# Side work of a hybrid decoder step resumed at estimated ready times, and x kept in scratch memory during the mixer

## The chip, the cores and the metric

The kernel runs on one core of one Trainium2 chip. It is one program that the core's engines work through in parallel: TensorE for matmuls (PE in the profile, with its weight loads as PEld), VectorE (DVE), ScalarE (ACT), GpSimd (POOL), and SyncE (SP), which issues most of the DMAs. Each engine takes its own instructions strictly in the order in which the program lists them, and waits where an operand isn't there yet. The metric is the device time of one execution in microseconds (us); lower is better.

## What is computed

One layer of a decoder for 512 prompt tokens and 8 sampled tokens (520 columns), in float32. Cut to what matters:

```python
def layer(x, ...):
    x = x + 0.5 * rmsnorm(swiglu(rmsnorm(x, ffn1_pre_g), gate1, up1, down1), ffn1_post_g)
    m, states = token_mixer(rmsnorm(x, mix_pre_g), ...)
    x = x + rmsnorm(m, mix_post_g)
    x = x + 0.5 * rmsnorm(swiglu(rmsnorm(x, ffn2_pre_g), gate2, up2, down2), ffn2_post_g)

def swiglu(x, w_gate, w_up, w_down):           # 1024 -> 2816 -> 1024
    return (silu(x @ w_gate) * (x @ w_up)) @ w_down

def token_mixer(h, ...):
    proj = h @ w_in                             # q, k, v, gates of two branches
    o_r = retention_chunked(rope(rq), rope(rk), rv)        # 4 heads of 128
    o_g = gated_delta_chunked(*conv_and_silu(conv_in))     # 4 heads of 128
    o_r = silu(rg) * normalized(o_r); o_g = silu(gz) * normalized(o_g)
    return (sigmoid(gate_r) * (o_r @ w_ret_branch) + sigmoid(gate_g) * (o_g @ w_gdn_branch)) @ w_out
```

The 8 sampled tokens go through the recurrent form of both branches: they read stored states, use them, and write them back updated.

## The kernel before, in words

**Matmuls.** Activations stand transposed, 128 channels by 520 tokens, in two halves of 260 columns. Each float32 product is made of three passes over numbers split into a high and a low part (L298 high by high, L299 high by low, L300 low by high; `passes`). These are the main stream: 9000 matmuls of 260 columns, whose order neither the tasks below nor the change touches. The names of their outputs tell the stage: `g` and `u` are the plain gate and up products at the start of an FFN, `sv` its further ones (seven products in place of eight for a pair of tiles), `dn` a down product or the mixer's output product, `p` the mixer's projections, `br` its branch products.

**Weights.** A weight tile is loaded to one of two `raw` buffers (L200 to L211, SP's queue), split on ACT (`whi`, L258) and on DVE or POOL (`wlo`, L259), for `sv` with `w` (L276, L277) from tiles of which some are first summed by POOL-issued DMAs that add in memory (L218). A `raw` buffer takes the next load when its `wlo` is done. SP's queue is in order: a load that waits for its buffer holds back every load and store behind it. I number the tiles ("units") of a stage from 0; `prefetch` splits about two units ahead, unless `hold` or `hold_sums` is set.

**Side work.** Everything else is written as generators: the RMS norms, the conv, the heads, the state updates. `tick()` is called after every second k-step of the main stream (6 matmuls) and advances every task whose step count has come: `yield 4` in a task means "resume four ticks later". So the place of a side instruction between the main matmuls is set by constants such as `yield 14` in `begin`, `yield 8` and `yield 13` in `gates`, `yield 9 + (0 if h else 6)` in `gdn_head`. They set the program's order only; what really happens on the chip is that an engine stops at an instruction whose operand is late.

**The RMS norm between two stages.** `post` finishes a stage: it gets the row sums by eight or four thin matmuls (`ss`, L360), a root on POOL (`rs`, L355), spreads it (`rb`, L366), and makes the new x half by half: DVE `t` (L492), POOL adds it to x (L494), ACT and DVE split it (`xhl`, L389, L390). `pre_rms` squares x (ACT, L407), adds the squares (DVE, L435) and starts `inverse_rms`: `ss` again, `ms` on DVE (L351), `rs`, sixteen `rb` in all, two copies (ACT L452, DVE L450). The result `r` scales every first product of the next stage when it leaves PSUM; the main stream begins that stage's products with `xhl` before `r` is there, and keeps them in PSUM banks (8 in all). `hold` is set in `post` and was cleared at the end of `pre_rms`, so that no weights are split in between except on demand; `hold_sums` is cleared at the end of `inverse_rms`.

**x.** x (8 tiles) stays in SBUF slots through the mixer, and is stored to a scratch tensor `x2` only for the second FFN, whose down stage loads it again (L623 in `down`, given `x_from`).

The functions in question, with the line numbers of the profile:

Of the kernel before, what the change touches and what calls it, by code (L numbers as in the profile page):

```python
# [7 lines left out]
F32 = mybir.dt.float32  # L8
# [7 lines left out]
P = 128  # L16
# [83 lines left out]

class Kernel:
    def __init__(self, ctx, tc, a):
        self.tc, self.nc, self.a = tc, tc.nc, a
        nc = tc.nc
        pool = lambda name, **kw: ctx.enter_context(tc.tile_pool(name=name, **kw))
        self.cpool = pool("const", bufs=1)
        self.big = pool("big", bufs=SLOTS)
        self.raw = pool("raw", bufs=RAW_BUFS)
        self.whl = pool("whl", bufs=SPLIT_BUFS)
        self.wk = pool("wk", bufs=2)  # L110
        self.sm = pool("small", bufs=8)
        self.ps = pool("ps", bufs=8, space=PSUM)
        self.dram = pool("scratch", bufs=1, space=DRAM)
        self.n = 0
        self.unit_list = units()
# [17 lines left out]
        self.loaded = {}  # L133
        self.split_done = {}
# [16 lines left out]
    def tick(self):  # L151
        self.now += 1
        self.add_sums()
        self.prefetch()
        for t in list(self.tasks):
            if t[0] <= self.now:
                try:
                    t[0] = self.now + (next(t[1]) or 1)
                except StopIteration:
                    self.tasks.remove(t)  # L160

# [28 lines left out]

    def load_to(self, j):

        nc, a = self.nc, self.a
        while self.raw_next < min(self.group[min(j, len(self.unit_list))] + RAW_BUFS, self.group[-1]):
            u = self.unit_list[self.first_of[self.raw_next]]
            if u[0] == "seven":
                w, m = a[f"gu{u[1]}"], u[2]
                t = self.raw.tile([P, KD, P], F32, tag="raw", name=self.name("raw"))
                s1, s3, a22 = (self.slot(x, (P, KH, P)) for x in ("s1", "s3", "a22"))
                nc.sync.dma_start(out=t, in_=w[2 * m])  # L200
                nc.sync.dma_start(out=s1, in_=w[2 * m + 1, :, 0:KH])
                nc.sync.dma_start(out=s3, in_=w[2 * m, :, 0:KH])
                nc.sync.dma_start(out=a22, in_=w[2 * m + 1, :, KH:KD])

                self.sums_due.append((self.now + SUM_LAG, self.raw_next, s1, w[2 * m + 1, :, KH:KD]))
                self.sums_due.append((self.now + SUM_LAG, self.raw_next, s3, w[2 * m + 1, :, 0:KH]))
                t = [t[:, 0:KH], s3, None, a22, t[:, KH:KD], s1, None]
            else:
                kind, m, k0, k1 = u
                t = self.raw.tile([P, k1 - k0, P], F32, tag="raw", name=self.name("raw"))  # L210
# [160 lines left out]
    def rstd(self, acc, scale, wait, plus, meanwhile=None):  # L371
# [39 lines left out]
    def pre_rms(self, xs, r, plus):  # L411
# [15 lines left out]
        yield 2  # L427
        yield from self.inverse_rms(sq[0], r, plus)
        self.hold = False
# [7 lines left out]
    def inverse_rms(self, acc, r, plus):  # L437
# [7 lines left out]
        yield 2  # L445
# [11 lines left out]
    def post(self, y, acc, hf, gnext, xs, r, plus, plus_next):  # L457
# [5 lines left out]
        yield 1  # L463
        meanwhile = (lambda: self.clear.append(1)) if hf else (lambda: self.prefetch(True, 1))
        r2 = yield from self.rstd(
            acc, 1.0 / D, 2 if gnext is None else 3, plus and plus[0:PW, hf * PIECES : (hf + 1) * PIECES], gnext is not None and meanwhile or None
# [242 lines left out]
    def run(self):  # L709
# [44 lines left out]
        def begin():  # L754
            yield 14
# [4 lines left out]
        xs, r = self.mixer(xs, r, plus2)  # L760
        x2 = self.dram.tile([P, KD, TOK], F32, name="x2")

        def keep():
            while len(xs[1]) < KD or r[1] is None:
                yield 1
            for k in range(KD):
                nc.sync.dma_start(out=x2[:, k, :], in_=self.x[k])
                yield 1

        self.spawn(keep())  # L770
        self.ffn(PLAIN[2], xs, r, V_G2PRE, self.gh[:, 8:16], None, plus2, None, x2)
        self.finish()

    def load_first(self):

        nc, a = self.nc, self.a
        t = self.raw.tile([P, KD, P], F32, tag="raw", name=self.name("raw"))
# [15 lines left out]
    def mixer(self, xs, r, plus_next):  # L793
# [33 lines left out]
        self.dec_done = set()  # L827
        tiles, gate, lead = {}, {}, {}
# [70 lines left out]
        return self.down(yx, (8,), self.vec[:, V_MPOST : V_MPOST + 8], V_G2PRE, 3, None, plus_next)  # L899
# [42 lines left out]
    def gates(self, rows):  # L942

        nc, c = self.nc, self.cpool
        yield 4
# [14 lines left out]
        yield 8  # L960
# [23 lines left out]
        yield 13  # L984
# [69 lines left out]
    def silu_later(self, t):  # L1054
        yield 5
        self.nc.scalar.activation(t, t, AF.Silu)

# [276 lines left out]
    def finish_head(self, kind, h, sg):  # L1334

        nc = self.nc
        yield 1
        nc.scalar.activation(sg, sg, AF.Silu)
        sgd = self.cpool.tile([P, DEC], F32, name=self.name("sgd"))
        yield 2  # L1340
# [4 lines left out]
        yield 6  # L1345
# [20 lines left out]
    def rsqrt(self, src, n, scale, name, out):  # L1366

        nc = self.nc
        ps = self.bank("cs")
# [5 lines left out]
        yield 5  # L1375
# [5 lines left out]
    def broadcast_rows(self, cols, name):  # L1381

        nc = self.nc
        pt = self.bank("tr32")
# [5 lines left out]
        return d  # L1390

    def state_update(self, rows, k, src, decay, out):

        nc = self.nc
        for i in range(8):
# [6 lines left out]
            yield 14  # L1402
            decay(s, h, b0)
            yield 4
# [12 lines left out]
    def state_products(self, src, rhs, n):  # L1417
# [4 lines left out]
        yield 10  # L1422
        for i in range(8):
            s, nxt = nxt, self.load_state(src, i + 1) if i < 7 else None
            ps = self.bank("sp")
# [3 lines left out]
            yield 7  # L1429
        self.prod = acc  # L1430

    def decode_ret(self):
# [7 lines left out]
        acc = self.prod  # L1440
        t = c.tile([P, H, DEC], F32, name="rdo")
# [5 lines left out]
        yield 2  # L1447
# [4 lines left out]
        yield 2  # L1452
# [4 lines left out]
        rows = self.broadcast_rows(v.rearrange("p h b -> p (h b)"), "vrow")  # L1457
        yield 6
# [6 lines left out]
    def decode_gdn(self):  # L1465
# [17 lines left out]
        yield 6  # L1483
# [9 lines left out]
        tt(qk, kn, kq[:, :, :, 1], ALU.mult)  # L1493
        yield from self.state_products(self.a["sgdn"], lambda h, b: kq[:, h, b, :], 2)
# [14 lines left out]
        yield 4  # L1509
# [4 lines left out]
        rows = self.broadcast_rows(u.rearrange("p h b -> p (h b)"), "urow")  # L1514
        yield 6
# [119 lines left out]
```

## Time and profile before

| | |
|---|---|
| device time, three runs | 1293.72, 1294.5, 1299.86 us (median 1294.5) |
| the profiled execution | 1299.34 us, of which its span is 1297.3 us |
| PE busy, instructions | 1233.3 us (95%), x10061 |
| DVE busy | 866.5 us (67%), x1911 |
| ACT busy | 547.0 us (42%), x1127 |
| POOL busy | 317.2 us (24%), x410 |
| moved by DMA | 167.38 MB, mean 129 GB/s |

Times in views of the trace count from the span's start. In a row of the timeline the columns are start, duration, engine, line, operation, output<-inputs, shape, how often, and in brackets how long the engine had been idle and what ended that. A row of a table by stretches gives the stretch, its length, then busy time of PE, PEld, DVE, ACT and POOL, each with its number of instructions, then the granted clock of TensorE as a share of full speed, the share of the DMA engines and GB/s. A row of waits gives engine, output and line, what it waited for, total us, times, longest us. In the profile's list of DMA issues a row ends with the size of one and its median time from issue to landing.

The stages in the trace: first FFN from 0 to about 379 us, mixer to about 892, second FFN to the end.

### The profile page before, as it was taken

To read this page: it belongs to the slowest core of one execution; us is meant where nothing else is said; L and a number is where in the kernel's file an instruction comes from. 1 tells how busy PE (TensorE), PEld (TensorE's weight loads), DVE (VectorE), ACT (ScalarE), POOL (GpSimd) and SP (SyncE) were. 2 spreads that over 40 slices of the span, in tenths; PEclk is the share of its full clock that TensorE was granted. 3 is DMA by queue.
4 is the path that set the end of the run, shared out by engine and by line. 5 is a ranking of instruction groups with operands and counts; after the bars stand their busy time and mean duration, and the time that the engine had idled before them with its cause. 6 is when DMAs were issued, how large, how long until landed. Compare 5 with 4: busy or idle time off the path is not lost.

```text
span 1297.3 us, 25497 instructions
## 1 busy us (share of the span) xinstructions
PE 1233.3 (95%) x10061; PEld 1219.7 (94%) x10061; DVE 866.5 (67%) x1911; ACT 547.0 (42%) x1127; POOL 317.2 (24%) x410
## 2 busy tenths in 40 slices
PE   8899999999998997999999999998889999999995
PEld 7899999999988997989999999998889999999995
DVE  8888888642254887877687655446768887862334
ACT  6566655522233553212333343323546655542220
POOL 4111211000024359227512333403311111100003
PEclk8999999999997999899999999997889999999997
DMA  5677777243321233232333564321377777634321
GB/s 172 170 182 195 177 185 178 86 156 92 97 62 53 95 101 89 71 101 97 106 133 111 178 205 136 126 82 50 119 192 183 180 196 182 147 90 156 90 74 66
DMA packets 77127, 167.38 MB, mean 129 GB/s; under 512 B 14544, under 2 KB 20016, under 8 KB 77008
## 3 DMA queue, kind: packets, MB, share of 16 engines
q1 hardware_dynamic: 64432, 140.95, 33.9%
q0 software_dynamic: 12576, 24.81, 10.9%
q8 instruction: 79, 1.29, 0.4%
q14 instruction: 40, 0.33, 0.1%
HBM read 156.03 MB, written 9.70 MB: 128 GB/s over the span
## 4 chain that ended last, share of the span: by engine, by line
PE 71%; DVE 11%; POOL 5%; issue 4%; DMA 4%; ACT 3%; SPq 1%; POOLq 0%; ACTq 0%; DVEq 0%
PE sv L298 10%; PE sv L299 10%; PE sv L300 10%; PE dn L299 7%; PE dn L298 7%; PE dn L300 7%; PE p L298 4%; PE p L300 4%; PE p L299 4%; DVE wlo L259 2%; DMA s<-gu_in 2%; DVE cv L1048 1%; PE br L298 1%; PE br L299 1%; PE br L300 1%
## 5 line engine op out<-in xcount | busy, mean ns | idle before, releaser
L298 PE MATMUL p<-xhl,whi 128*128 128x260 f32 x784 | 237.5, 303 | 2.2 <-ACT whi L258 2.2
L300 PE MATMUL p<-xhl,wlo 128*128 128x260 f32 x784 | 227.8, 291 | 1.8 <-DVE wlo L259 1.0
L299 PE MATMUL p<-xhl,whi 128*128 128x260 f32 x784 | 228.3, 291 | 0.7 <-DVE xhl L390 0.6
L299 PE MATMUL dn<-hl,whi 128*128 128x260 f32 x704 | 199.6, 283 | 3.3 <-DVE hl L606 3.3
L298 PE MATMUL dn<-hh,whi 128*128 128x260 f32 x704 | 199.5, 283 | 0.0
L300 PE MATMUL dn<-hh,wlo 128*128 128x260 f32 x704 | 198.8, 282 | 0.0
L298 PE MATMUL sv<-th,w 128*128 128x260 f32 x608 | 173.2, 285 | 4.4 <-ACT u L638 4.3
L299 PE MATMUL sv<-tl,w 128*128 128x260 f32 x608 | 172.9, 284 | 0.0
L300 PE MATMUL sv<-th,w 128*128 128x260 f32 x608 | 172.9, 284 | 0.0
L298 PEld LDWEIGHTS p<-xhl,whi 128*128 128x128 f32 x784 | 154.5, 197 | 3.1 <-ACT whi L258 2.4
L259 DVE TENSOR_TENSOR wlo<-raw,whi 128x1024 fp32r<-128x1024 f32 (+2 forms) x107 | 116.4, 1105 | 60.4 <-ACT whi L258 60.0
L300 PEld LDWEIGHTS p<-xhl,wlo 128*128 128x128 f32 x784 | 154.1, 197 | 2.3 <-DVE wlo L259 1.2
L299 PEld LDWEIGHTS p<-xhl,whi 128*128 128x128 f32 x784 | 154.3, 197 | 1.6 <-DVE xhl L390 1.1
L258 ACT CAST whi<-raw 128x1024 fp32r<-128x1024 f32 (+2 forms) x137 | 126.7, 943 | 65.5 <-DMA raw<-dn_in 55.2
L218 POOL DMA_DIRECT2D s<-gu_in x76 | 67.1, 954 | 322.6 <-DMA s<-gu_in 149.1
L277 DVE TENSOR_TENSOR w<-s,w 128x512 fp32r<-128x512 f32 x152 | 104.5, 689 | 53.2 <-ACT w L276 52.1
L299 PEld LDWEIGHTS dn<-hl,whi 128*128 128x128 f32 x704 | 132.6, 188 | 4.1 <-DVE hl L606 4.1
L298 PE MATMUL sv<-xhl,w 128*128 128x260 f32 x456 | 129.4, 284 | 4.2 <-DVE t L617 4.2
L300 PEld LDWEIGHTS dn<-hh,wlo 128*128 128x128 f32 x704 | 132.6, 188 | 0.0
L298 PEld LDWEIGHTS dn<-hh,whi 128*128 128x128 f32 x704 | 132.6, 188 | 0.0
L299 PE MATMUL sv<-xhl,w 128*128 128x260 f32 x456 | 129.0, 283 | 0.0
L300 PE MATMUL sv<-xhl,w 128*128 128x260 f32 x456 | 128.9, 283 | 0.0
(362 smaller groups left out, 2990.8 us busy)
## 6 DMA issues: line engine op xcount, KB each, us to landing
raw<-gu_in SPq DMA_DIRECT2D x49, 512.0 KB, 3.7
raw<-win_in SPq DMA_DIRECT2D x49, 512.0 KB, 3.5
s<-gu_in SPq DMA_DIRECT2D x76, 256.0 KB, 4.2
s<-gu_in POOLq DMA_DIRECT2D x76, 256.0 KB, 4.8
raw<-dn_in SPq DMA_DIRECT2D x32, 448.0 KB, 3.5
a<-gu_in SPq DMA_DIRECT2D x38, 256.0 KB, 4.6
raw<-dn_in SPq DMA_DIRECT2D x16, 512.0 KB, 3.6
x<-x SPq DMA_DIRECT2D x16, 260.0 KB, 6.3
```

Source lines behind the costliest of these rows:

```text
L218: self.nc.gpsimd.dma_start(out=out, in_=term, accum_op=ALU.add)
L258: self.nc.scalar.copy(hi[:, ks], t[:, ks])
L259: eng.tensor_tensor(lo[:, ks], t[:, ks], hi[:, ks].bitcast(F32), ALU.subtract)
L277: nc.vector.tensor_tensor(w[:, 1], t[i], w[:, 0].bitcast(F32), ALU.subtract)
L298: mm(ps, hi[:, k, :], xh, start=first, stop=False, skip_group_check=more)
L299: mm(ps, hi[:, k, :], xl, start=False, stop=False, skip_group_check=more)
L300: mm(ps, lo[:, k, :], xh, start=False, stop=last, skip_group_check=more)
L1048: nc.vector.scalar_tensor_tensor(out=acc, in0=cin[:, j : j + SEQ], scalar=w[:, j : j + 1], in1=acc, op0=ALU.mult, op1=ALU.add)
```

## The change

A class `Clock` sees every instruction while the program is built. It keeps, with constants for each engine, an estimate of when each engine comes free and when each tile is written. `at(tiles)` gives the estimated ready time of tiles; a task that yields it is resumed by `tick` once the estimate of PE's time has reached it. `raw_tile` tells it when SP's queue has to wait for a `raw` buffer. Most fixed counts before an instruction of PE become such times. Nothing of it runs on the chip: what changes there is the order of the instructions.

```diff
+class At(float):
+    step = 1 << 30
+class Clock:
+    FIXED = {"DVE": 75.0, "ACT": 110.0, "POOL": 160.0}
+    TAIL = 90.0
+    COLUMN = {"DVE": 1.04, "ACT": 0.79, "POOL": 2.2}
+    HANDOVER = 120.0
...
+    def note(self, ins):
...
+        start = max([self.free[engine]] + [self.ready(x) + self.HANDOVER for x in args])
...
+        elif engine == "PE":
+            self.count += 1
+            full = all("float32r" in str(x.dtype) for x in args)
+            self.free[engine] = start + (cols / 2.4 + 11.0 if full else max(60.0, 4 * cols / 2.4))
+            end = self.free[engine] + 170.0
+        else:
+            column = 1.35 if ins.opcode == "TensorScalarPtr" and len(args) > 2 else self.COLUMN[engine]
+            self.free[engine] = start + self.FIXED[engine] + column * cols
+            end = self.free[engine] + self.TAIL
...
     def tick(self):
...
+        clock = self.clock
+        if clock.count == self.seen:
+            clock.free["PE"] += 300.0
+        self.seen = clock.count
         for t in list(self.tasks):
-            if t[0] <= self.now:
+            if t[0] <= clock.free["PE"] or t[0].step <= self.now if isinstance(t[0], At) else t[0] <= self.now:
                 try:
-                    t[0] = self.now + (next(t[1]) or 1)
+                    wait = next(t[1])
+                    t[0] = wait if isinstance(wait, At) else self.now + (wait or 1)
...
+    def at(self, *aps, within=None):
+        t = At(max(self.clock.ready(x) for x in aps) + self.clock.HANDOVER)
...
     def rstd(...):
-        yield wait
+        yield self.at(r[0:PW])
     def pre_rms(...):
         self.add_squares(1)
-        yield 2
+        self.hold = False
+        yield self.at(sq[0])
         yield from self.inverse_rms(sq[0], r, plus)
-        self.hold = False
     def inverse_rms(...):
-        yield 2
+        yield self.at(s[0:PW])
     def begin():
-        yield 14
+        yield self.at(self.sq[0])
     def gates(...):
-        yield 4
+        yield self.at(rows[0:8])
...
-        yield 8
+        yield self.at(ga, gb)
...
-        yield 13
+        yield self.at(beta, g)
     def silu_later(self, t):
-        yield 5
+        yield self.at(t)
     def gdn_head(...):
-        yield 9 + (0 if h else 6)
+        while k.name not in self.silued or q.name not in self.silued:
+            yield 1
+        yield self.at(k, q)
     def rsqrt(...):
+        yield self.at(src)
         ps = self.bank("cs")
     def state_products(...):
-        yield 10
+        yield 4
         for i in range(8):
             s, nxt = nxt, self.load_state(src, i + 1) if i < 7 else None
+            yield self.at(s)
...
-            yield 7
+            yield 4
     def run(self):
...
-        xs, r = self.mixer(xs, r, plus2)
-        x2 = self.dram.tile([P, KD, TOK], F32, name="x2")
+        x1, x2 = (self.dram.tile([P, KD, TOK], F32, name=n) for n in ("x1", "x2"))
+        self.spawn(self.keep(x1, xs, r))
+        xs, r = self.mixer(xs, r, plus2, x1)
+        self.spawn(self.keep(x2, xs, r))
```

The same is done in `finish_head`, `broadcast_rows`, `state_update`, `decode_ret`, `decode_gdn` and at the start of `post`. The heads' inner steps (`ret_head`, `inverse`, the chunk loop of `gdn_head`) keep their counts. `keep` stores the eight x tiles to `x1` after the first FFN, and the mixer's output stage loads them back (16 more DMAs of 260 KB); nothing else is added to or taken from any engine.

What it does to the order is shown at two places. The first is the end of the norm between the first FFN and the mixer, on ACT (units 2, 3, 4 and 5 of the mixer's weights are `whi` in this order; `early` is an evacuation, `rb` the copy of the first half of `r`). Before:

```order
L407 ACTIVATE sq_4827<-x_3865 128x260
L258 CAST whi_5101<-raw_4696 128x256 x4
L542 COPY early_4907<-p_5020 128x260
L452 COPY rb_5160<-rb_5161 128x260
L258 CAST whi_5179<-raw_4916 128x1024
L258 CAST whi_5185<-raw_5111 128x1024
L258 CAST whi_5215<-raw_5183 128x1024
```

And on ACT with the change:

```order
L503 ACTIVATE sq_4821<-x_3865 128x260
L354 CAST whi_5097<-raw_4696 128x256 x4
L354 CAST whi_5122<-raw_4925 128x1024
L638 COPY early_4916<-p_5029 128x260
L354 CAST whi_5143<-raw_5107 128x1024
L354 CAST whi_5204<-raw_5126 128x1024
L548 COPY rb_5230<-rb_5231 128x260
```

The high parts of units 3, 4 and 5 now stand ahead of the copy of `r`. POOL follows: its low parts of units 3 and 4 stood behind the root `rs`, and now stand ahead of it; on DVE the low part of unit 5 has moved from behind the copy L450 to just ahead of it. On PE the second `ss` stands 36 main matmuls later and the `rb` 48 later. At the norm between mixer and second FFN it is 36 and 42 (POOL's `wlo` of unit 3 ahead of `rs`, and on DVE the `wlo` of unit 4 ahead of `ms`).

The second place is on DVE in the second FFN, where the first weights of the `sv` products are split (`w`, `s`) between the token sums (`xd`, `ta`, `tb`, `tl`: four groups). Before:

```order
L571 TENSOR_TENSOR tl_11717<-tb_11694,th_11716 128x520
L606 TENSOR_TENSOR hl_11703<-h_11585,hh_11702 128x520
L259 TENSOR_TENSOR wlo_11722<-raw_11634,whi_11721 128x1024
L277 TENSOR_TENSOR w_1901_11733<-raw_11640,w_1901_11733 128x512
L277 TENSOR_TENSOR w_1904_11746<-s_1875_11642,w_1904_11746 128x512
L272 SCALAR_TENSOR_TENSOR s_1905_11749<-s_1874_11641,raw_11640 128x512
L277 TENSOR_TENSOR w_1906_11751<-s_1905_11749,w_1906_11751 128x512
L562 TENSOR_TENSOR xd_11764<-x_3861 128x260
```

And on DVE with the change:

```order
L662 SCALAR_TENSOR_TENSOR tb_11720<-x_10901,vec,tb_11720 128x260
L713 TENSOR_TENSOR t_11728<-early_11370,rb_11705 128x260
L373 TENSOR_TENSOR w_1896_11740<-raw_11597,w_1896_11740 128x512
L373 TENSOR_TENSOR w_1897_11743<-s_1867_11599,w_1897_11743 128x512
L368 SCALAR_TENSOR_TENSOR s_1898_11746<-s_1866_11598,raw_11597 128x512
L373 TENSOR_TENSOR w_1899_11748<-s_1898_11746,w_1899_11748 128x512
L667 TENSOR_TENSOR tl_11753<-ta_11719,th_11752 128x520
```

The block that reads the summed tiles stood behind the third of the four groups; now it stands inside the second, so one and a half groups more are behind it. On SP the loads for it now stand ahead of all eight stores to `x2`; before, one store stood ahead of them, five right behind, and two behind the next tiles' loads.

In the mixer, the thin matmul of the decode branch (`cs`, L1370) stands 36 main matmuls later, the four delta heads' chains 30 later; the sixteen groups of state products (`sp`) stand up to 48 later or up to 102 earlier.

More of the change, by code (lines that the diff above doesn't have):

```diff
@@ L114, in __init__ @@
         self.n = 0
+        self.clock = Clock()
+        nc.push_inst_callback(self.clock.note)
+        self.seen = 0
         self.unit_list = units()
@@ L188, in dbank, with raw_tile @@
         return self.bank(name)[:, 0:n]
+    def raw_tile(self, shape):
+        t = self.raw.tile(shape, F32, tag="raw", name=self.name("raw"))
+        self.raws.append(t)
+        if len(self.raws) > RAW_BUFS:
+            clock = self.clock
+            clock.free["SP"] = max(clock.free["SP"], clock.read.get(self.raws[-1 - RAW_BUFS].name, 0.0))
+        return t
     def load_to(self, j):
@@ L759, in run, with keep @@
         xs, r = self.ffn(PLAIN[1], xs, r, V_G1PRE, self.gh[:, 0:8], V_MPRE, plus1, None, a["xT"])
[L760 to L770 removed]
+        x1, x2 = (self.dram.tile([P, KD, TOK], F32, name=n) for n in ("x1", "x2"))
+        self.spawn(self.keep(x1, xs, r))
+        xs, r = self.mixer(xs, r, plus2, x1)
+        self.spawn(self.keep(x2, xs, r))
         self.ffn(PLAIN[2], xs, r, V_G2PRE, self.gh[:, 8:16], None, plus2, None, x2)
         self.finish()
+        nc.pop_inst_callback()
+    def keep(self, out, xs, r):
+        x = self.x
+        while len(xs[1]) < KD or r[1] is None:
+            yield 1
+        for k in range(KD):
+            self.nc.sync.dma_start(out=out[:, k, :], in_=x[k])
+            yield 1
     def load_first(self):
         nc, a = self.nc, self.a
[L777 removed]
+        t = self.raw_tile([P, KD, P])
         self.loaded[0] = t
```

92 lines of the change are left out of this document (70 added, 22 removed).

## The prediction

> **What bounds the kernel.** I read the totals first, then a table by stretches, then who PE waits for, and then the timeline around the longest waits.
>
> ```profile
> span 1297.3 us, 25497 instructions
> PE 1233.3 (95%) x10061; PEld 1219.7 (94%) x10061; DVE 866.5 (67%) x1911; ACT 547.0 (42%) x1127; POOL 317.2 (24%) x410
> PE 71%; DVE 11%; POOL 5%; issue 4%; DMA 4%; ACT 3%; SPq 1%; POOLq 0%; ACTq 0%; DVEq 0%
> ```
>
> PE is the bound: 64 us of the span are its idle time, and its share of the chain is 71%. But busy isn't the same as at full speed. The table by stretches shows where speed is lost:
>
> ```profile
> 0.00:62.00 62.00, 52.89 (x375) 50.65 (x376) 50.10 (x92) 37.07 (x79) 19.76 (x29) 0.89 0.64 178
> 62.00:372.00 310.00, 308.27 (x2572) 307.82 (x2572) 197.99 (x365) 142.28 (x274) 27.90 (x32) 1.00 0.54 146
> 372.00:420.00 48.00, 41.44 (x273) 40.07 (x273) 26.55 (x59) 18.93 (x44) 22.48 (x21) 0.79 0.16 48
> 420.00:490.00 70.00, 69.92 (x588) 69.49 (x588) 55.67 (x131) 38.07 (x95) 34.56 (x46) 1.00 0.30 92
> 490.00:585.00 95.00, 81.77 (x645) 79.53 (x645) 79.07 (x232) 26.75 (x60) 43.73 (x75) 0.91 0.30 91
> 585.00:700.00 115.00, 111.88 (x982) 109.57 (x982) 88.10 (x286) 36.50 (x82) 54.07 (x94) 0.99 0.34 108
> 885.00:965.00 80.00, 67.03 (x449) 64.69 (x449) 57.25 (x116) 39.25 (x87) 24.51 (x26) 0.81 0.41 116
> ```
>
> From 62 to 372 PE runs without a break: 310 us for 2572 matmuls, 0.12 us each, at full clock. Four stretches lose time: the start, the norm at 372 to 420, the mixer from 490 on, and the norm at 885 to 965. Who ends PE's waits:
>
> ```profile
> PE cs L1370 <- DVE gsq L1482: 5.6, 1, 5.6
> PE ss L360 <- DVE sq L435: 5.3, 2, 2.7
> PE sv L298 <- ACT u L638: 4.3, 2, 3.4
> PE sv L298 <- DVE t L617: 4.2, 1, 4.2
> PE sp L1427 <- DMA sd<-sret_in: 1.0, 1, 1.0
> PE ss L360 <- DVE sq L751: 0.9, 1, 0.9
> ```
>
> The first two are side instructions that stand on PE ahead of their operands, with main matmuls queued behind them. The change moves exactly these: both `ss` and the `cs` stand 36 main matmuls later. The next two are main matmuls that wait for a PSUM bank. No task's place can cure those unless DVE and ACT get there sooner.
>
> **The change, part by part.** The estimate runs while the program is built, and costs nothing on the chip. Each instruction of before is there again; 16 DMAs are added.
>
> *The norm after the first FFN.*
>
> ```profile
> 404.67 1.04 PE L360 MATMUL ss<-ones,sq 128*65 128x1 f32 x8 [2.66 <-DVE sq L435]
> 403.60:417.10 13.50, 12.43 (x61) 12.43 (x62) 1.54 (x5) 2.27 (x3) 6.34 (x3) 0.50 0.17 66
> 417.20:430.70 13.50, 13.50 (x115) 13.32 (x115) 9.71 (x23) 4.36 (x6) 0.67 (x4) 1.00 0.26 80
> 401.41 3.20 DVE L435 TENSOR_TENSOR sq<-sq,sq 128x260 f32<-128x260 f32 x7
> 405.99 1.64 POOL L355 TENSOR_TENSOR rs<-ms,mhalf 65x8 f32<-65x8 f32 x1 [7.11 <-DVE ms L351]
> 410.43 1.99 ACT L258 CAST whi<-raw 128x1024 fp32r<-128x1024 f32 x2
> 411.55 4.70 POOL L259 TENSOR_TENSOR wlo<-raw,whi 128x1024 fp32r<-128x1024 f32 x2 [3.92 <-ACT whi L258]
> 418.65 1.23 DVE L259 TENSOR_TENSOR wlo<-raw,whi 128x1024 fp32r<-128x1024 f32 x1 [6.36 <-ACT whi L258]
> 419.80 0.75 DVE L939 TENSOR_TENSOR rows<-early,rb 8x260 f32<-8x260 f32 x2
> ```
>
> PE stops at 402.0 for squares that are done at 404.6. Then the clock is 0.50 for 13.5 us, 61 instructions where the next 13.5 us hold 115. With the change PE does 36 main matmuls instead (4.3 us, to 406.3), by which time the squares are done: `ss` to 406.9, `ms` by 407.1. POOL is the doubtful step: `whi` of unit 3 can go at 401 (ACT is free, `hold` is cleared), its `wlo` takes 2.35 from 402.1; unit 4's raw load goes out as the squares begin, at 401.5, and needs 3.5 (below), `whi` to 406.1, `wlo` to 408.5, and only then `rs`, 1.64, to 410.1. PE reaches `rb` 24 matmuls after `ss`, at 409.8, so it waits 0.3 and ends the sixteen at 411.8. PE is then 48 matmuls further (5.7 us) at the same time as before, and at full clock where before ran at half until 417.1: 8 us.
>
> What is late next is DVE. It stood idle for 6.36 us to 418.65, because unit 5's `whi` waited for a raw buffer that POOL's late `wlo` held, and first uses `r` at 419.80. With the change unit 5 is loaded at 404.5 and split by 410.5, and DVE uses `r` from 412.3: 7.5 us sooner. From 420 to 490 DVE is busy 55.7 of 70, and the rest is a 0.7 us wait inside each conv, so it carries PE's lead no further than its own. I take **7.5**, with 3 to 8 as bounds.
>
> The clock is the larger part of that lead: 8 us at 0.50, of which PE's own wait is 2.66. The Trainium skill ("TensorE: Matmul & The Clock Gate", section "HAM oscillation — how this bites in real kernels") puts the rule as no PE-idle gaps over about 3.4 us. By that rule a gap of 2.66 us would not be enough; the half clock did begin with it here, so the row differs from the rule, and the row decides. What the rule leaves open is a rival below.
>
> *The mixer.*
>
> ```profile
> 489.24 0.29 DVE L1159 TENSOR_TENSOR cols<-se,rr 128x4 f32<-128x4 f32 x1 [3.19 <-POOL rr L1150]
> 514.04 0.17 DVE L1159 TENSOR_TENSOR cols<-se,rr 128x4 f32<-128x4 f32 x1 [1.71 <-POOL rr L1150]
> 516.99 0.23 DVE L1482 TENSOR_TENSOR gsq<-dcv 128x64 f32<-128x64 f32 x1 [0.35 <-ACT dcv L1479]
> ```
>
> PE waits 5.6 us at `cs` for `gsq`, done at 517.2, and DVE gets there late because it is the bound: from 490 to 585 it is busy 79 of 95, and of the rest 3.19 and 1.71 us are waits for POOL's `rr`, which the change doesn't touch. The 36 matmuls now ahead of `cs` fill 4.3 of the 5.6. But PE comes some 8 us sooner and `gsq` only 7.5, so part of the wait stays. From 490 to 700 PE idles 16.4 us by the two rows of the stretches, so 10.8 beside `cs`, and the granted clock of 0.91 and 0.99 costs about 0.09 x 95 + 0.01 x 115 = 9.7. Those are the waits of the chunk loops, whose tasks keep their counts; only their neighbours move. I take **5**: the filled 4.3, and a little of the rest. Bounds: -3 (DVE is in the way of all that it gained), +11 (half of the waits and of the slow clock go).
>
> *The norm before the second FFN.*
>
> ```profile
> 920.39 0.63 PE L360 MATMUL ss<-ones,sq 128*65 128x1 f32 x8 [2.68 <-DVE sq L435]
> 937.16 0.95 POOL L218 DMA_DIRECT2D s<-gu_in  x1 [8.06 <-DMA s<-gu_in]
> 945.80 0.62 ACT L276 CAST w<-s 128x512 fp32r<-128x512 f32 x1 [6.97 <-DMA s<-gu_in]
> 946.46 0.69 DVE L277 TENSOR_TENSOR w<-s,w 128x512 fp32r<-128x512 f32 x1 [5.93 <-ACT w L276]
> 954.09 0.75 DVE L617 TENSOR_TENSOR t<-g,rb 128x260 f32<-128x260 f32 x2
> ```
>
> The same gap goes, and PE would be some 8 us ahead. But the first `sv` waits for the bank that `t` frees at 954.8, and `t` stands on DVE behind splits that wait for summed tiles. With the change those tiles' loads are issued about 8 us sooner (their buffers come free at 923 where it was 931) and no `x2` stores share the DMA with them, so by the 4.8 us of such a load (below) the two or three additions of a tile are through near 934, not 945.7. Yet on DVE the waiting split now stands one and a half token groups earlier, so more is behind it: splits 2.6, what is left of group two 1.5, `h` 0.7, groups three and four with their waits 3.4 + 3.1, `hl` 0.6, splits 1.8, `t` 0.8, from starts in before: 14.5 us. That ends at 949.0, not 954.8. PE then waits about 6 us at `sv`. I take **6**, between 2 and 9 (PE's lead and the wait after it).
>
> *The start.*
>
> ```profile
> 25.00:45.00 20.00, 18.67 (x159) 18.46 (x160) 18.84 (x37) 10.99 (x21) 3.94 (x3) 1.00 0.48 123
> 28.49 0.77 PE L366 MATMUL rb<-cst,rs 65*128 65x65 f32 x5 [1.10 <-POOL rs L355]
> 59.03 0.58 PE L298 MATMUL sv<-th,w 128*128 128x260 f32 x1 [3.39 <-ACT u L638]
> 55.58 1.14 ACT L276 CAST w<-s 128x512 fp32r<-128x512 f32 x2 [2.64 <-DMA s<-gu_in]
> ```
>
> `ss` waited 0.9 us here (the row of the squares of L751 above) and `rb` 1.1; they move by 24 and 36 matmuls. PE then meets DVE, busy 18.8 of the 20 us from 25 to 45. Of the 3.39, ACT's 2.64 for a summed tile goes (splits come sooner, so its buffer does). I take **3**, 0 to 5.
>
> *x to scratch.*
>
> ```profile
> raw<-win_in SPq DMA_DIRECT2D x49, 512.0 KB, 3.5
> x<-x SPq DMA_DIRECT2D x16, 260.0 KB, 6.3
> s<-gu_in POOLq DMA_DIRECT2D x76, 256.0 KB, 4.8
> ```
>
> Six of the eight stores stand on SP between two raw loads, at about 409, where the DMA engines are 17% busy. They may hold the second load back by 6 us; it is needed 10 us later. The loads at the mixer's end stand ahead of one `wo` tile, split two units (11 us) ahead. I cost both at nothing; without that cover, 3 us each. These lie inside the bounds.
>
> **Sum.** 7.5 + 5 + 6 + 3 = 21.5. Against the profiled 1299.34 (span 1297.3 and 2.0 around it) that is 1277.8; that run is 4.8 above the median, so for the median of 1294.5 I say **1273**. All lows give 3 - 3 + 2 + 0 = 2, all highs 33.
>
> **Rivals.** *DVE keeps its time* (0.17): 3 + 0 + 3 + 3 = 9, 1285.5. For it: 79 of 95 us in the mixer; against it: its 6.36 us of idle time. *The waits only change places* (0.18): `rs` behind two `wlo` on POOL, a split ahead of the token groups; each would take back what its norm gains, and what is left is 1288 to 1301. For it: both moves are there; against it: their times above. *PE loses in the state products* (0.06): sixteen `sp` groups, each waiting on PE for a state load that stands on SP behind raw loads. If eight came 3.5 us (one landing) late, each with a stretch at half clock that costs 1.7, that is 42 us, less 21.5: 1315. It decides from 28 us of new waits on. Against it: before, `sp` waited 1.0 us on such a load, once. *The half clock comes from the thin `ss` and `rb` themselves* (0.05): they are in the row of 61 instructions too, and the change keeps them. Then PE's lead in a norm is the 2.7 us of the gap, not 7.5, and the mixer and the second norm are entered with that: 4.8 less, 16.7 in all, 1278. For it: the clock falls as they begin; against it: the gap stands there as well, and the start ran `ss` and `rb` after waits of 1 us with the clock at 1.00 (25 to 45 above). *The mixer's slow clock goes too* (0.08): 33 us, 1261.5. The forecast, 1264 to 1283, has 0.46.
>
> 0.5% is 6.5 us, about what a measurement of this kernel can tell from no change: faster is below 1288. That gives 0.76 faster, 0.18 same, 0.06 slower. The range that leaves out the state products and a part of the second rival is 1258 to 1291.
>
> **What will show it.** Right: no wait at `ss` in either norm, the clock near 1.00 from 403 to 417, `rows` on DVE 7 us sooner, a shorter but present wait at `cs`, `t<-g` near 949 less the earlier lead, PE still waiting there. Wrong: PE waiting at `rb` for POOL, DVE's `rows` no sooner, `sp` among PE's longest waits, or raw loads held back behind the x stores.

## The result and the profile after

| | before | with the change |
|---|---|---|
| median of 14 runs each | 1296.76 us | 1304.38 us |
| lowest, highest | 1292.72, 1301.88 | 1300.58, 1310.48 |
| profiled execution, its span | 1299.34, 1297.3 | 1306.56, 1304.8 |

The ratio is 1.0059, with a 95% interval from 1.0042 to 1.0076: the change makes the kernel 0.6% **slower**, where 1.7% faster was predicted. The totals of the page of after:

```profile
span 1304.8 us, 25528 instructions
PE 1231.9 (94%) x10061; PEld 1217.9 (93%) x10061; DVE 879.2 (67%) x1911; ACT 545.8 (42%) x1127; POOL 319.5 (24%) x410
PE 66%; DVE 15%; issue 6%; DMA 4%; POOL 4%; ACT 3%; SPq 1%; POOLq 0%; DVEq 0%; ACTq 0%
```

The engines execute as many instructions as before, yet DVE is busy 879.2 us in place of 866.5, and its share of the chain of work went from 11% to 15%, PE's from 71% to 66%. The same stretches as in the prediction, with after's own rows:

```profile
372.00:420.00 48.00, 42.09 (x308) 41.22 (x307) 31.94 (x66) 19.32 (x45) 23.41 (x22) 0.86 0.30 89
420.00:490.00 70.00, 68.36 (x561) 67.94 (x560) 57.64 (x123) 36.58 (x94) 33.31 (x38) 0.98 0.31 95
490.00:585.00 95.00, 81.89 (x648) 78.74 (x647) 79.00 (x233) 27.37 (x61) 46.17 (x82) 0.91 0.30 91
585.00:700.00 115.00, 108.00 (x932) 105.17 (x930) 90.21 (x277) 38.05 (x90) 50.96 (x92) 0.97 0.37 122
885.00:965.00 80.00, 67.08 (x496) 65.52 (x495) 56.46 (x116) 37.08 (x81) 24.48 (x25) 0.85 0.42 123
```

The two norms got better (308 matmuls where there were 273, 496 where there were 449); the mixer got worse: 561 for 588, and from 585 to 700 932 for 982. Who ends PE's waits now:

```profile
PE u L394 <- DVE h L720: 8.1, 2, 5.8
PE sv L394 <- ACT u L734: 5.3, 2, 3.5
PE po L1210 <- DVE st L1218: 4.8, 2, 3.4
...
PE ss L456 <- DVE sq L531: 3.0, 2, 2.5
...
PE pS L1326 <- DVE AT L1323: 2.5, 2, 1.4
...
PE pX L1431 <- DVE pack L1427: 2.3, 1, 2.3
PE sp L1533 <- DMA sd<-sret_in: 2.2, 1, 2.2
...
PE cs L1474 <- DVE gsq L1589: 0.3, 1, 0.3
```

The wait at `cs`, the longest of before with 5.6 us, is gone. In its place stand waits that before didn't have among its longest: `u` for `h`, `po` for `st`, `pX`, `pS`, and `sp` for a state load. The wait at `ss` in the first norm is still there.

**How the stages are compared.** The main stream has the same 9000 matmuls in the same order in every kernel here; I number them from 0. So the start of the n-th in one trace can be subtracted from its start in another. The table gives, for places where the side work of the norm beside them is done, how much later (+) a kernel is than before's profiled run, and so what a stage gained or lost:

| main matmul, stage it ends | before, us | after, us | difference |
|---|---|---|---|
| 138, norm at the start | 34.7 | 31.7 | -3.0 |
| 259, `u` products ahead of the first `sv` | 49.1 | 50.2 | +1.1 |
| 2964, first FFN (and 24 matmuls of the mixer) | 388.7 | 391.9 | +3.2 |
| 3102, first norm | 419.9 | 417.6 | -2.4 |
| 4819, heads and decode branch | 736.7 | 745.5 | +8.8 |
| 6084, mixer's output (and 24 of the second FFN) | 902.6 | 913.8 | +11.2 |
| 6390, second norm | 963.6 | 971.1 | +7.5 |
| 8999, second FFN | 1280.4 | 1288.1 | +7.8 |

The first norm gained 5.6 us and the second 3.7. Between 3102 and 4819 PE lost 11.2. Each number is from one execution, and between kernels whose edits don't touch a stage it differs by up to 4 us (the first FFN, from 259 to 2964, loses from 1.9 to 6.0 in every kernel but e4). So what is read below is what recurs.

### The profile page after: what moved, and what is told of

It reads as the page before. It is cut to its first block, busy times and chain, and to the rows that moved or that the text cites. A ratio compares the mean times of both kernels' runs of the same rounds, so it can differ in the third digit from the quotient of the medians.

```text
span 1304.8 us, 25528 instructions
## 1 busy us (share of the span) xinstructions
PE 1231.9 (94%) x10061; PEld 1217.9 (93%) x10061; DVE 879.2 (67%) x1911; ACT 545.8 (42%) x1127; POOL 319.5 (24%) x410
## 4 chain that ended last, share of the span: by engine, by line
PE 66%; DVE 15%; issue 6%; DMA 4%; POOL 4%; ACT 3%; SPq 1%; POOLq 0%; DVEq 0%; ACTq 0%
PE sv L394 10%; PE sv L395 10%; PE sv L396 10%; PE dn L395 6%; PE dn L394 6%; PE dn L396 6%; PE p L394 4%; PE p L396 4%; PE p L395 4%; DVE wlo L355 2%; DMA s<-gu_in 2%; DVE cv L1148 2%; PE br L394 1%; PE br L395 1%; PE br L396 1%
```

## The experiments

Fifteen kernels were run, each against before on the same chip; there were four chips, with medians of before from 1299.24 to 1301.33 us, so ratios and not times are compared. Most of them are the changed kernel with one part put back. The ratios are to before, with the 95% interval; the columns behind them are stage gains (-) and losses (+) as above, from the profile.

| kernel | ratio | first norm | mixer, 3102 to 4819 | second norm |
|---|---|---|---|---|
| the change | 1.0059 (1.0042 to 1.0076) | -5.6 | +11.2 | -3.7 |
| e1 `hold` back | 1.0145 (1.0127 to 1.0163) | -2.5 | +9.6 | +10.0 |
| e2 mixer's counts back | 0.9949 (0.9933 to 0.9966) | -5.7 | -0.9 | -3.1 |
| e3 x stays | 1.0046 (1.0029 to 1.0064) | -6.5 | +13.5 | -1.4 |
| e4 norms' counts back | 1.0077 (1.0060 to 1.0093) | 0.0 | +10.8 | -1.1 |
| e5 chains back | 1.0017 (0.9991 to 1.0043) | -3.8 | +6.1 | -6.0 |
| e6 decode branch back | 1.0040 (1.0023 to 1.0057) | -5.8 | +10.2 | -5.1 |
| e7 state products back | 0.9995 (0.9979 to 1.0011) | -10.1 | +4.4 | -3.0 |
| e8 = e2 and `wlo` on DVE | 0.9923 (0.9904 to 0.9942) | -10.5 | -1.8 | -2.3 |
| e9 gates back | 1.0066 (1.0039 to 1.0093) | -8.1 | +15.7 | -1.2 |
| e10 load estimate 4.3 us | 0.9991 (0.9971 to 1.0010) | -7.2 | +9.8 | -3.3 |
| e11 parts kept | 0.9924 (0.9900 to 0.9949) | -10.6 | +0.4 | -4.8 |
| e12 = e11, sums split later | 0.9879 (0.9855 to 0.9904) | -8.4 | +0.7 | -8.4 |
| e13 heads' start back | 1.0037 (1.0024 to 1.0050) | -10.1 | +9.4 | -2.8 |
| e14 `finish_head` back | 1.0088 (1.0070 to 1.0105) | -5.7 | +12.1 | -1.2 |
| e15 estimate and norms | 0.9932 (0.9916 to 0.9948) | -12.9 | +7.7 | -8.6 |

### Where the time went: norms, mixer, x

e2 puts back every count of the mixer's tasks (those of the diff from `gates` to `state_products`, and in the functions listed under it):

```diff
-        yield self.at(ga, gb)
+        yield 8
...
-            yield self.at(s)
             ps = self.bank("sp")
```

> The changed kernel, with all counts of the mixer's tasks put back (gates, silu, delta heads, finish_head, decode branch, state products); norms, `hold` and x scratch stay changed. Theory M (PE's new waits in the mixer, where PE fell back by some 8 us between 585 and 720): 6 to 10 us less than the changed kernel, 1294 to 1298 (ratio 0.998 to 1.002). Rival H or X (the loss is in the norms or in the x stores): 1302 to 1306.

Measured 0.9949, better than the 0.998 to 1.002 of theory M: the rest of the change is a gain of 0.5%, and the mixer's tasks cost 1.1%. e4 is the counterpart, with the norms put back and the mixer's tasks left as changed:

```diff
-        self.hold = False
-        yield self.at(sq[0])
+        yield 2
         yield from self.inverse_rms(sq[0], r, plus)
+        self.hold = False
```

> The changed kernel, with the counts of the norms put back (`post`, `pre_rms`, `inverse_rms`, `begin`, and `hold` cleared at the end); the mixer's tasks and the x scratch stay changed. Theory M (the mixer loses 8, the norms gain a few): slower than the changed kernel by 0 to 5, 1304 to 1310 (ratio 1.006 to 1.010). Rival H (the norms lose): 1297 to 1300, near before.

1.0077: the first norm gains nothing, the mixer loses 10.8 as in the change. The two agree: the norms gain, the mixer loses more. e3 takes `x1` away:

```diff
-        self.spawn(self.keep(x1, xs, r))
-        xs, r = self.mixer(xs, r, plus2, x1)
+        xs, r = self.mixer(xs, r, plus2, None)
```

> The changed kernel without `x1`: x stays in SBUF through the mixer, and the 16 DMAs are gone; the order on PE, DVE, ACT and POOL is the same. Theory X (the eight stores at 409 us hold back raw and state loads on SP, or the loads at the mixer's end do): 3 to 6 us less than the changed kernel, 1298 to 1301. If the stores are hidden, as the prediction had it: 1303 to 1305, ratio 1.005 to 1.007.

1.0046 against 1.0059, with intervals that overlap: the stores and loads are hidden, or nearly so.

### The first norm: two engines, one port

Why does PE still wait at `ss`, 36 matmuls later than before? After's timeline there, DVE, POOL and PE:

```profile
403.44 7.38 DVE L531 TENSOR_TENSOR sq<-sq,sq 128x260 f32<-128x260 f32 x7
404.01 2.56 POOL L355 TENSOR_TENSOR wlo<-raw,whi 128x1024 fp32r<-128x1024 f32 x1 [3.10 <-ACT whi L354]
408.20 2.34 POOL L355 TENSOR_TENSOR wlo<-raw,whi 128x1024 fp32r<-128x1024 f32 x1 [1.63 <-ACT whi L354]
411.79 2.56 POOL L451 TENSOR_TENSOR rs<-ms,mhalf 65x8 f32<-65x8 f32 x1 [1.25 <-DVE ms L447]
410.88 0.63 PE L456 MATMUL ss<-ones,sq 128*65 128x1 f32 x8 [2.54 <-DVE sq L531]
```

The seven additions of squares took 3.20 us before, and take 7.38 now. The view by tile gives their shortest, median and longest in ns, for the change, for e7 (in this place the same order) and for e8:

```profile
L531 DVE TENSOR_TENSOR sq<-sq,sq x7: 419/429/2539, 403.4 to 408.3; 128x260 f32<-128x260 f32 x7
```

```profile
L531 DVE TENSOR_TENSOR sq<-sq,sq x7: 422/428/2511, 402.1 to 406.9; 128x260 f32<-128x260 f32 x7
406.95 2.62 POOL L355 TENSOR_TENSOR wlo<-raw,whi 128x1024 fp32r<-128x1024 f32 x1 [1.75 <-ACT whi L354]
```

```profile
L531 DVE TENSOR_TENSOR sq<-sq,sq x7: 423/428/431, 400.3 to 403.0; 128x260 f32<-128x260 f32 x7
405.06 2.37 POOL L355 TENSOR_TENSOR wlo<-raw,whi 128x1024 fp32r<-128x1024 f32 x1 [7.34 <-ACT whi L354]
```

Most additions take 0.43 us even then; single ones take 2.5. They aren't slowed a little each, one of them stands still until the `wlo` is done. So the seven take 3.2, 5.3 or 7.4 us with no, one or two `wlo` begun just ahead of one of them; no other length was seen in the first norm of any kernel here. In all traces together 27 additions of the two norms stand so, and each ends 0.28 to 0.29 us behind the end of a `wlo` that began 0.06 to 0.36 us ahead of it. In the change the last addition starts at 408.3, just behind POOL's second `wlo` at 408.20, and stands. In e7 it starts at 406.9, just ahead of POOL's at 406.95, and goes through. Less than a tenth of a microsecond decides over 2.1, and the first norm's gain is 5.6 in the one and 10.1 in the other. Over the kernels with the norms as changed it is 3.8 to 7.2 where the seven take 7.4 us, 8.1 to 10.1 where they take 5.3 (e7, e9, e13), and 8.4 to 12.9 where they take 3.2 (e8, e11, e12, e15; e1, with `hold` back, is the exception below). The Trainium skill ("SBUF — State Buffer", section "🔬 SBUF: two separate sides") describes it as an exclusive lock: VectorE and GpSimd share one pair of ports, and the one that starts first keeps it for its whole instruction. These rows agree: the stop lasts until the `wlo` is over.

e8 moves the low parts of unit 3, of the mixer and of the second FFN, from POOL to DVE, on top of e2:

```diff
-        self.on_pool = {kinds.index("win") + n for n in (3, 4)} | {kinds.index("gu2") + 3}
+        self.on_pool = {kinds.index("win") + 4}
```

> The kernel with the mixer's counts back (0.9949), and beside it the low parts of `win` unit 3 and of `gu2` unit 3 on DVE in place of POOL, so that no POOL `wlo` runs beside the seven additions of squares. If POOL's `wlo` is what stretches the additions from 3.2 to 7.4 us, they take 3.2 again in both norms, PE's wait of 2.5 us at `ss` goes, and with the half clock behind it 3 to 6 us: ratio 0.990 to 0.993. If the additions stay long, or DVE's own 1.2 us for the low parts cost as much: 0.994 to 0.997.

0.9923 against e2's 0.9949; the intervals just overlap, and the first norm's gain in the profiles is 10.5 against 5.7. The additions take 3.2 us, the wait at `ss` is gone, and the half clock with it, as the row of before's bad stretch shows in after and in e8:

```profile
403.60:417.10 13.50, 10.96 (x89) 10.87 (x88) 8.32 (x9) 2.90 (x5) 7.47 (x3) 0.87 0.59 175
```

```profile
403.60:417.10 13.50, 13.03 (x118) 12.82 (x117) 7.22 (x17) 3.58 (x5) 4.34 (x4) 1.00 0.63 206
```

e8 runs the same thin `ss` and `rb` in it, at a clock of 1.00, and so do e11, e12 and e15: these matmuls alone did not halve it. But the gap alone doesn't settle it either. e3 has the gap too (2.58 us), and the same stretch there is at 1.00; and in e8 PE has no gap from 434.7 to 438.4, where it does the 26 small matmuls of the gates, and yet runs at half clock from 437.04:

```profile
403.60:417.10 13.50, 10.92 (x101) 10.84 (x101) 9.28 (x13) 2.57 (x4) 6.46 (x3) 1.00 0.55 157
```

```profile
437.04:440.45 3.41, 3.41 (x17) 3.41 (x18) 3.41 (x4) 0.81 (x3) 3.41 (x3) 0.50 0.18 26
```

So around `ss` and `rb` of the first norm the half clock came only in kernels with a gap there, not in each of them, and elsewhere it came without one.

e1 asked whether clearing `hold` early is worth having:

```diff
-        self.hold = False
         yield self.at(sq[0])
         yield from self.inverse_rms(sq[0], r, plus)
+        self.hold = False
```

> The changed kernel, with `hold` cleared only after `inverse_rms`, as before. Theory H (POOL's two `wlo`, let ahead of the root, run beside DVE's seven additions of squares, which took 7.4 us where before they took 3.2, so that PE still stops 2.5 us at `ss` though `ss` stands 36 matmuls later): the additions take 3.2 again in both norms, the wait at `ss` and the 3.4 us at half clock behind it go, 4 to 6 us less than the changed kernel, about 1299 (ratio to before 1.002). Rival M (the loss sits in the mixer's side work): the additions are short, but the time stays at 1302 to 1305 (1.005), because the mixer uses up any lead.

1.0145: a clear miss. The additions were short (3.20), as theory H had it, and yet it is the slowest kernel of all. Its waits say why:

```profile
PE u L394 <- DVE h L720: 12.5, 2, 11.7
...
PE p L396 <- POOL wlo L355: 3.2, 1, 3.2
```

With `ss` and `rb` later, `hold` holds the splits back longer too, and PE runs out of split weights (`p` for `wlo`) and, in the second norm, waits 11.7 us for `h`. So the later `ss` needs `hold` cleared early; what e8 shows to do harm is POOL's part of it.

### The mixer: which tasks?

e5, e6 and e7 put back the heads' chains, the decode branch, and of that only the state products:

```diff
 def state_products(...):
-        yield 4
+        yield 10
...
-            yield self.at(s)
...
-            yield 4
+            yield 7
```

> The changed kernel, with the counts of before in the heads' chains alone (`gates`, `silu_later`, `gdn_head`, `finish_head`); decode branch, state products, norms, `hold` and x scratch stay changed. Putting all of the mixer's counts back was worth 1.1% (1.0059 to 0.9949). Theory C (the delta heads' chains now stand where DVE is late: PE waits at `gc`, `pX`, `pS`, `tr`, `po`, and `br` for the last head): most of it comes back, ratio 0.995 to 0.999. Rival D (decode branch and state products): 1.003 to 1.006.

> The changed kernel, with the counts of before in the decode branch alone (`rsqrt`, `broadcast_rows`, `state_update`, `decode_ret`, `decode_gdn`, `state_products`); the heads' chains stay changed. Theory C: the 5.6 us wait at `cs` is back, little is won, ratio 1.003 to 1.008. Rival D: 0.995 to 0.999.

> The changed kernel, with the counts of before in `state_products` alone (10 ahead, 7 between, no wait for the estimate). If the one wait at `sp` for a state load (2.2 us and half clock for 6.8 us behind it) costs what it seems, 5 us come back: ratio 1.002. If the heads' chains use that time up again: 1.005 to 1.007.

1.0017, 1.0040 and 0.9995. Theory C has part of it (the mixer loses 6.1 and not 11.2), and so have the products (4.4; 4.5 us more of the gain in e7's profile is the lucky start of POOL's `wlo` above). e6, which puts the products back too, still loses 10.2: the parts don't add. Where the loss lies is told by the same comparison at two more main matmuls, 4100 and 4300:

| kernel | 3102 to 4100 | 4100 to 4300 | 4300 to 4819 |
|---|---|---|---|
| the change | +2.1 | +5.8 | +3.2 |
| e5 chains back | +1.5 | -0.7 | +5.3 |
| e6 decode branch back | +2.9 | +6.1 | +1.3 |
| e7 state products back | +0.6 | +1.3 | +2.5 |

Half of it lies between 4100 and 4300, and goes with the chains put back as well as with the products: it takes both. It is seen on SP, then PE, in the change:

```profile
SPq L1362 <- DVE AT L1285: 14.2, 4, 5.9
```

```profile
633.63 1.76 SPq L1362 DMA_DIRECT2D s<-AT  x4
639.02 0.42 SPq L1519 DMA_DIRECT2D sd<-sret_in  x1
```

```profile
644.45 0.37 PE L1533 MATMUL sp<-rdec,sd 128*128 128x1 f32 x1 [2.21 <-DMA sd<-sret_in]
```

A delta head's `AT` is late on DVE, SP stands at its store for it, the state load behind that is issued at 639.0, lands 5.4 us later, and PE stands at `sp`. The granted clock is 0.50 from 644.5 to 651.3. That is the rival of the state products, once instead of eight times. In e6 PE waits 3.4 us at such a load and 2.8 at another, though the products have the counts of before; in e7, with the chains moved as well, it waits at none. Why it does in e6 isn't shown.

e9, e13 and e14 put single parts of the chains back: the gates; the start of a delta head; `finish_head`.

```diff
 def gdn_head(...):
-        while k.name not in self.silued or q.name not in self.silued:
-            yield 1
-        yield self.at(k, q)
+        yield 9 + (0 if h else 6)
```

> The changed kernel, with the counts of before in `gates` alone (4, 8, 13); all else of the mixer stays changed. In the changed kernel PE waits 1.6 us at `gc` for `gg`, because on DVE the gate rows now stand behind a conv that takes 4.3 us beside POOL's `wlo`, and 3.4 us at half clock follow; PE falls back by 3 us between 432 and 458. If that place is what the gates cost: no wait at `gc`, 2 to 4 us less, ratio 1.002 to 1.004. If the mixer uses any lead up later: 1.005 to 1.007.

> The changed kernel, with the counts of before where a delta head starts (`silu_later` 5, `gdn_head` 15 and 9); all else of the mixer stays changed. Putting all the chains' counts back gave 1.0017 for 1.0059, the gates alone 1.0066. Theory P (the heads' later start shifts their DVE work ahead of the retention state `st`, for which PE now waits 4.8 us at `po`, and 0.8 with all counts back): the waits at `po` fall below 1.5 us, ratio 1.001 to 1.004. Rival F (the last steps of a head, `finish_head`, cost it): 1.005 to 1.007.

> The changed kernel, with the counts of before in `finish_head` alone (1, 2, 6). Theory P: nothing is won, the waits at `po` stay at 4 us or more, 1.005 to 1.007. Rival F: the waits at `br` and at `tr` for `go` (2.1 and 1.3 us) go, ratio 1.001 to 1.004.

1.0066, 1.0037, 1.0088: no single part is the cause, and with `finish_head` back it is slower than either theory had it. With the gates put back the wait at `gc` is gone, and others took its place:

```profile
PE po L1210 <- DVE st L1218: 7.2, 3, 3.0
PE pV L1405 <- DVE pack L1381: 7.0, 1, 7.0
...
PE tr L1034 <- ACT cv L1156: 3.0, 1, 3.0
```

e13 comes out in the range of theory P, but not by its reason: `po` still waits 5.3 us, its mixer still loses 9.4 where the change loses 11.2, and 4.5 us of its profile's gain are the first norm's, with additions of 5.3 us. What is shown is that the chains lose time together (e5), not in which order of DVE's work it arises. That stays open.

e11 keeps the decode branch as changed (the `cs` with its 36 matmuls), with chains and products put back and e8's `wlo`:

> The norms, `hold`, the x scratch and the decode branch as changed; the counts of before in the heads' chains and in the state products; the low parts of `win` 3 and `gu2` 3 on DVE. If the parts add up (0.9923 with the whole mixer put back, and the rest of the decode branch worth up to 0.45%): 0.987 to 0.991. If the decode branch gains only where the chains lose: 0.991 to 0.994.

0.9924, the same as e8 within intervals of 0.25% to each side. The filled wait at `cs` was worth nothing: it moved on to the next side instruction that needs DVE. e8 waits 5.6 us at `cs` and 1.4 at `pV`, e11 7.7 at `pV`:

```profile
PE u L394 <- DVE h L720: 7.9, 2, 6.7
PE pV L1403 <- DVE pack L1379: 7.7, 1, 7.7
```

e10 changes one constant of the estimate:

```diff
-            end = max(start + 1900.0, self.dma + 1500.0)
+            end = max(start + 4300.0, self.dma + 1500.0)
```

> The changed kernel, with one constant of the estimate changed: a load is taken to land 4.3 us after its issue, as the state loads do in the trace (4.3 and 4.9 median), in place of 1.9. If the tasks are resumed too early because the estimate is short for loads: no wait at `sp`, and 3 to 6 us less, ratio 1.001 to 1.003. If the load was late because it stood on SP behind `s<-AT`, which waited 5.5 us for DVE, the constant doesn't cure it: a wait at `sp` of 1 us or more stays, ratio 1.005 to 1.008.

0.9991, better than theory, though the wait at `sp` falls to 1.0 us and isn't gone. Between 4100 and 4300 it loses 0.2 us in place of 5.8, but in the rest of the mixer 4.3 more than the change. So only 1.4 of its profile's gain of 6.3 at the end lies in the mixer, the rest in stretches that vary between profiles, and how much of it is the constant's own is not settled.

### The second norm

In after the block that waits for the summed tiles stands on DVE ahead of `h`, and PE's `u` behind `h`:

```profile
947.69 0.69 DVE L373 TENSOR_TENSOR w<-s,w 128x512 fp32r<-128x512 f32 x1 [7.44 <-ACT w L372]
951.50 0.76 DVE L720 TENSOR_TENSOR h<-g,s 128x260 f32<-128x260 f32 x2
```

```profile
951.97 0.58 PE L394 MATMUL u<-xhl,whi 128*128 128x260 f32 x1 [5.76 <-DVE h L720]
```

e12 adds to e11 a flag that holds this block back until the third token group is done:

```diff
-            if seven and self.hold_sums and not force:
+            if seven and (self.hold_sums or self.hold_split) and not force:
...
             F["B22"].append(xs[1][k + KH])
+            if k == 2:
+                self.hold_split = False
```

> The kernel e11, and beside it the block of splits that waits for the summed tiles stands on DVE behind the third of the token groups in the second FFN, as it did before the change, and not inside the second. PE waited 7.0 us at `u` for `h`, which stood behind that block. If the block's place is the cause: no wait at `u`, and 3 to 6 us less than e11, ratio 0.983 to 0.988. If the wait only moves on to `sv` for `t`: within 2 us of e11.

0.9879 against e11's 0.9924 on the same chip. DVE does `h` at 925.72, ahead of the block, and then waits 2.98 us for the tiles, where after's DVE waited 7.44:

```profile
925.72 0.76 DVE L723 TENSOR_TENSOR h<-g,s 128x260 f32<-128x260 f32 x2
...
933.67 0.69 DVE L374 TENSOR_TENSOR w<-s,w 128x512 fp32r<-128x512 f32 x1 [2.98 <-ACT w L373]
```

PE's wait at `u` in the second FFN is gone, and 3.8 us remain at `sv` for `t`. It is the fastest kernel here, 1.2% below before.

Last, e15 leaves every task as changed and corrects the rest: the load time of the estimate, the two `wlo`, the place of the block.

> The changed kernel with every task of it left as changed, and three corrections: a load is taken to land after 4.3 us in the estimate (0.9991 alone), the low parts of `win` 3 and `gu2` 3 on DVE, and the waiting block behind the third token group. If the corrections of the norms are worth what they were with the mixer put back (0.26% and 0.45%): 0.990 to 0.994, above e12's 0.988. If the mixer uses their lead up: 0.995 to 0.999.

0.9932. The corrections of the norms are worth what they were in e12 (second norm -8.6 and -8.4), and the mixer still loses 7.7.

## Why the prediction was wrong, point by point

**The step that failed is the mixer's term**, "I take 5: the filled 4.3, and a little of the rest", and above it the words "whose tasks keep their counts; only their neighbours move". It measured a loss of 11.2. The lower bound, -3, supposed at worst that DVE is in the way of all that it gained. But the change also moves the delta heads' starts, the gates and the state products on DVE and SP, in a stage in which DVE is busy 79 of 95 us, and each resumed at its own estimated time. What e2 shows is that these moves cost 12 us together: its mixer gains 0.9 where the change's loses 11.2. Two places are seen in the trace. The 6.8 us that the change wins at `cs`, between main matmuls 3640 and 3730, come back as 10.8 lost between 3800 and 3990, where PE waits at `po` and `pS` for DVE; and 5.8 go between 4100 and 4300, with the wait at `sp`. That no single part of the chains makes up the loss is shown by e9, e13 and e14; which order of DVE's work starts it stays open.

**The filled wait at `cs`** came as predicted (0.3 us left of 5.6), and gave nothing: e11 and e8 have the same time. That is the rival *DVE keeps its time*, stated for this reason and costed at zero in the mixer, not at a loss.

**The first norm**: 7.5 predicted, 5.6 measured. The time came, by another way than described: "by which time the squares are done" was wrong, since they were done at 410.8 and not at 404.6: they began 2.0 us later than before, and took 4.2 longer. The two `wlo` were put ahead of the root on POOL as the prediction said, and their 2.3 us each were counted there; what they do to DVE was not. "no wait at `ss`" was one of the marks of being right, and it failed, as did "`rows` on DVE 7 us sooner" (418.14 against 419.80). Without the collision the norm gains 8.4 to 12.9 (e8, e11, e12, e15), more than predicted.

**The second norm**: 6 predicted, 3.7 measured. The fault in the order was seen ("on DVE the waiting split now stands one and a half token groups earlier") and its cost computed for `t` and `sv`; that the bank of `h`, which stands behind the split too, stops PE at `u` was missed, and that is the 5.76 us. e12 shows the size: 0.45%.

**The start**: 3 predicted. The norm itself gained 3.0; at main matmul 259, ahead of the first `sv`, all was gone. The wait at `sv` for ACT's `u` has the same length as before (3.5 and 3.4), and a new one at `u` for `h` of 2.3 us, the rest of the 8.1 above, stands ahead of it. Another 2.1 us went in the first FFN and 2.4 in the mixer's output stage, for which the sum has no term; no run tells whether the change costs them.

**x to scratch** at nothing: held within what e3 can tell.

**The rivals.** The waits did change places, in the mixer above all, and further than that rival went: its upper end, 1301, is below the result. The state products had the right place and queue, and one occurrence where the rival needed eight. That `ss` and `rb` halve the clock by themselves is excluded by e8. The range, up to 1291, left out the products and a part of the other, and no term of the sum was bounded below -3; in the mixer the waits that moved cost more than the filled one brought.

## What to carry to other kernels

A wait that was filled on the leading engine was worth nothing here, because the engine behind it stayed the bound: ask which of its instructions is late next, and count the moved tasks on that engine, not only on the one that waited. When an order is set by an estimate, the estimate needs what the chip adds to a duration: with two engines on one port, less than a tenth of a microsecond decided here whether an addition stood still, and a load takes its traced time (4.3 and 4.9 us for the states) and not an assumed one (1.9). Judge such a change part by part: here one half gained 0.5% and the other lost 1.1%, and the total showed neither.

## What the runs showed of the hardware that was not expected

An addition of 128x260 on VectorE took 0.43 us or 2.5 us, in the views above, according to whether a GpSimd subtraction of 128x1024 had begun ahead of it and was still running. And the stretch at half clock behind a gap varied: 13.5 us followed a gap of 2.66 us before, and behind a gap of 2.54 us in the same place after it was 3.4 (0.72 granted from 411.00 to 417.10, below). In e3 it was none behind 2.58 us, and in e8 a stretch of 3.4 us came with no gap at all (their rows are above). What sets it isn't shown.

```profile
411.00:417.10 6.10, 6.10 (x44) 6.10 (x45) 1.31 (x2) 0.57 (x2) 2.56 (x1) 0.72 0.74 213
```
